# 48 units of u loaded ahead, gathers of u in steps 5 to 121 with up to seven buffers, each row multiplied one step after its fetch

## The chip, the cores and the metric

The kernel runs on one core of a Trainium2 chip. The metric is the device time of one execution in microseconds (us), taken as the median of several runs.

## The reference, cut to what matters

The kernel is one decoder layer over 256 tokens of width 2048. After an attention part and a LayerNorm, a retrieval part ("PEER") picks 128 experts for each token (8 heads of 16) out of 16384 and applies them:

```python
qh = (xc @ wq).reshape(PEER_CHUNK, PEER_HEADS, 2, PEER_HALF)
s1 = jnp.einsum('thd,kd->thk', qh[:, :, 0], sub_keys[0]).astype(jnp.float32)
s2 = jnp.einsum('thd,kd->thk', qh[:, :, 1], sub_keys[1]).astype(jnp.float32)
v1, i1 = lax.top_k(s1, PEER_TOPK)
v2, i2 = lax.top_k(s2, PEER_TOPK)
...
best, pos = lax.top_k(cand, PEER_TOPK)
expert = jnp.take_along_axis(cidx, pos, axis=-1)
gate = jax.nn.softmax(best, axis=-1)
u_sel = u[expert]
v_sel = v[expert]
act = jax.nn.gelu(jnp.einsum('td,thkd->thk', xc, u_sel).astype(jnp.float32), approximate=False)
return jnp.einsum('thk,thkd->td', (gate * act).astype(x.dtype), v_sel)
```

The change concerns the product of each token with the selected rows of u.

## The kernel before, in words

The product with u is made in two ways at once. For the first 1408 of the 2048 columns TensorE multiplies all tokens with all rows of u (the dense part). For the last 640 columns only the selected rows are fetched, by indirect DMA, and VectorE multiplies them with the token (the gathered part).

**The W_Q stage** comes first: 48 units (tiles of 128x512 floats, 256 KB each) of the query weights stream through four buffers named raw. Each unit is split into a high part (ScalarE, `hi`, L94) and a low part (`lo`, L95, on VectorE or, for units of odd number here, on GpSimd), and TensorE multiplies the tokens with both. In the same stretch VectorE and GpSimd find the best sixteen of each head (`retrieve`).

**The u stage** has 128 steps. A step takes 11 blocks of u, that is 2.75 units; 352 units in all. Each unit is split as above into one of four hi/lo pairs, each block takes three matmuls, and at the end of a step ScalarE copies the step's result from PSUM into the large tile S (L680). S has 64 places of one unit each; a place is filled with results as every second step ends, and until then it can hold a unit of u that was loaded ahead. A small planner (`place`, `follow`) decides when each unit is loaded into which place: a place may take a unit again once the one before it has been split, and only if no result is due there until the unit is used. The planner loads some units already in the W_Q stage (`PRE`), and two for each consumed unit after that as long as places are free. The last `RAW_END` units don't go through S but through the four raw buffers (L104).

**The gathers** are 256 indirect DMAs of 320 KB (128 rows of 640 floats), issued by GpSimd (L659) and spread evenly over the steps from `G0` up to `GE`. Their buffers rotate in the order of the program: `GB` = 3 of their own, and `GR` of every `GB + GR` from the raw buffers. VectorE multiplies each with the tokens' last 640 columns and sums (L684). The instructions that follow `issue_after` on VectorE may not stand ahead of the step's last split.

Loads are issued by SyncE in one queue; a load that waits for its buffer holds up those behind it. The framework orders each engine's instructions beforehand by an estimate of its own; loads and splits have a raised priority. After the u stage come the extraction of the gathered products and a stage of the same kind for v.

The knobs of the change: `PRE = (1, 2)` (a load ahead after every second W_Q unit), `RAW_END = 24`, `GR = 2`, `G0 = 12`, `GE = 125`.

Of the kernel before, what the change touches and what calls it, by code (L numbers as in the profile page):

```python
# [31 lines left out]
GU = D - KDU * P  # L32
# [6 lines left out]
UNIT = 512  # L39
EB = 8  # L40
GB = 3
GR = 2
GR_END = 128
RB = 4
RAW_END = 24
FIRST = 2
EARLY = 4
POOL_U = (1, 3)
# [1 line left out]
POOL_UE = 20  # L50
EARLY0 = 16
EARLY_N = 2
PRE = (1, 2)
BP = 3
AHEAD = 3000
G0 = 12
GE = 125
LEAD = 5
LAG = 1
KEEP0 = 40  # L60
# [11 lines left out]
def layer(ctx, tc, A, out):  # L72
# [11 lines left out]
    def bankA(name):  # L84
        return psA.tile([P, 512], F32, name=name, tag="a")
# [14 lines left out]
    def load_unit(src, raw=None, eng=None):  # L100
        with tc.high_priority(offset=AHEAD):
            if raw is None:
                raw = raw_unit()
                last_load[0] = nc.sync.dma_start(raw, src).ins  # L104
            pair = tuple(stream.tile([P, UNIT], F32R, name=s, bufs=4) for s in ("hi", "lo"))
            split(pair[0], pair[1], raw, eng)
        return pair
# [10 lines left out]
    def mm3(o, l, r, first, last):  # L118
        mm(o, l[0], r[0], start=first, stop=False)  # L119
        mm(o, l[0], r[1], start=False, stop=False)  # L120
        return mm(o, l[1], r[0], start=False, stop=last).ins  # L121
# [374 lines left out]
    def step_of(i2, sl=slice(0, T)):  # L496
        return S[:, i2 // 2, sl.start // 2:sl.stop // 2, i2 % 2, :]
# [4 lines left out]
    def s_part(p):  # L502
        return S[:, p].rearrange("p a b c -> p (a b c)")

    def paired(a):
        return a.rearrange("p (t j) -> p t j", j=2)
# [7 lines left out]
    for m in range(-WQ_UNITS, U_UNITS):  # L514
# [3 lines left out]
        n = max(n, m + 1)  # L518
        for _ in range((m * PRE[0] % PRE[1] < PRE[0]) if m < 0 else 2):
            fit = [p for p in free if 2 * p > (4 * n + 3) // KDU + 1]  # L520
            if n < U_UNITS - RAW_END and fit:
                place[n] = min(fit)
# [4 lines left out]
    def load_ahead(m):  # L527
        for n in follow[m]:
            p = place[n]
            with tc.issue_after(last_load[0]):  # L530
                last_load[0] = nc.sync.dma_start(s_part(p), A["u_d"][n]).ins

    count = [-WQ_UNITS]
# [117 lines left out]
    gorder = [(tt, h * PK + k) for h in range(HEADS) for k in range(PK) for tt in range(NT)]  # L651

    def gather(table, tt, slot, n):
        if table is A["u_g"] and slot < GR_END and count[0] % (GB + GR) >= GB:
            g = stream.tile([P, n], F32, name="g", tag="raw", bufs=RB)
        else:
            g = gath.tile([P, n], F32, name="g", bufs=GB)
        count[0] += 1
        nc.gpsimd.indirect_dma_start(out=g, out_offset=None, in_=table,  # L659
                                     in_offset=bass.IndirectOffsetOnAxis(ap=e_idx[:, tt, slot:slot + 1], axis=0))  # L660
        return g

    def spread(i, i0, i1):
        n = i1 - i0
        return gorder[len(gorder) * min(max(i - i0, 0), n) // n:len(gorder) * min(max(i - i0 + 1, 0), n) // n]

    after_unit[0] = None
    count[0] = 0
    w = None
    for i2 in range(P):  # L670
        ps = bankA("ups")[:, :T]
        for kt in range(KDU):
            un, k = divmod(i2 * KDU + kt, 4)
            if k == 0:
                p = place.get(un)
                w = load_unit(A["u_d"][un], None if p is None else s_part(p),
                              nc.gpsimd if un < POOL_UE and un % 4 in POOL_UU else None)
                load_ahead(un)
            mm3(ps, tuple(a[:, k * P:(k + 1) * P] for a in w), hs[kt], kt == 0, kt == KDU - 1)
        nc.scalar.copy(step_of(i2), paired(ps))  # L680
        with tc.issue_after(last_split[0]):
            for tt, slot in spread(i2, G0, GE):
                g = gather(A["u_g"], tt, slot, GU)
                nc.vector.scalar_tensor_tensor(g, g, 1.0, h_gath[:, tt], op0=ALU.mult, op1=ALU.mult,  # L684
                                               accum_out=pd[:, tt, slot:slot + 1])

# [92 lines left out]
    for m in range(P * NC):  # L779
        v_follow[m] = []  # L780
        i2, c = divmod(m, NC)
# [172 lines left out]
```

## Time and profile before

| what | value |
|---|---|
| median of 3 runs | 1747.99 us (1747.92 to 1755.24) |
| the profiled execution | 1756.99 us, span 1755.2 us |
| granted TensorE clock, mean | 0.984 |
| TensorE matmul busy | 1666.4 us (95%) |
| VectorE busy | 1450.0 us (83%) |
| ScalarE busy | 897.5 us (51%) |
| GpSimd busy | 886.7 us (51%) |
| the first and the last result copy of the u stage | at 500.30 and 1019.50 us |

The profile shows a single execution, whose own time is 9 us above the median. Busy times are shares of the whole span; the stages have different limits, so the u stage has to be read by itself.

### The profile page before, as it was taken

To read this page: it belongs to the slowest core of one execution; us is meant where nothing else is said; L and a number is where in the kernel's file an instruction comes from. 1 tells how busy PE (TensorE), PEld (TensorE's weight loads), DVE (VectorE), ACT (ScalarE), POOL (GpSimd) and SP (SyncE) were. 2 spreads that over 40 slices of the span, in tenths; PEclk is the share of its full clock that TensorE was granted. 3 is DMA by queue.
4 is the path that set the end of the run, shared out by engine and by line. 5 is a ranking of instruction groups with operands and counts; after the bars stand their busy time and mean duration, and the time that the engine had idled before them with its cause. 6 is when DMAs were issued, how large, how long until landed. Compare 5 with 4: busy or idle time off the path is not lost. (4 is left out here: it accounts for less than half of the span.)

```text
span 1755.2 us, 33099 instructions
## 1 busy us (share of the span) xinstructions
PE 1666.4 (95%) x10652; PEld 1484.7 (85%) x10652; DVE 1450.0 (83%) x3515; ACT 897.5 (51%) x1885; POOL 886.7 (51%) x899
## 2 busy tenths in 40 slices
PE   8999999989899999999999889988999999999996
PEld 8999888869888999999999788876687888888883
DVE  6766676679999888889888798877888888889896
ACT  6545565444344555555554358773454555555551
POOL 0000000036775656566565588856747645456562
PEclk9999999989999999999999999998999999999998
DMA  7667657726688999999999841137999999999962
GB/s 219 179 188 192 203 175 261 255 79 214 193 287 268 337 361 321 323 347 336 344 330 329 293 146 55 55 103 255 296 329 333 381 338 332 338 319 328 352 200 89
DMA packets 206014, 451.13 MB, mean 257 GB/s; under 512 B 26928, under 2 KB 31472, under 8 KB 205328
## 3 DMA queue, kind: packets, MB, share of 16 engines
q1 hardware_dynamic: 164816, 297.93, 51.4%
q0 software_dynamic: 41024, 151.09, 24.7%
q8 instruction: 84, 1.38, 0.3%
q14 instruction: 90, 0.74, 0.1%
HBM read 444.59 MB, written 4.26 MB: 256 GB/s over the span
## 5 line engine op out<-in xcount | busy, mean ns | idle before, releaser
L94 ACT CAST hi<-S 128x512 fp32r<-128x512 f32 x677 | 420.4, 622 | 450.5 <-PE vacc L121 223.2
L95 DVE TENSOR_TENSOR lo<-S,hi 128x512 fp32r<-128x512 f32 x672 | 464.5, 701 | 89.6 <-ACT hi L94 81.4
L121 PE MATMUL ups<-hTh,lo 128*128 128x256 f32 x1408 | 392.2, 283 | 11.7 <-DVE lo L95 11.1
L119 PE MATMUL ups<-hTh,hi 128*128 128x256 f32 x1408 | 392.2, 280 | 4.5 <-ACT hi L94 4.2
L120 PE MATMUL ups<-hTl,hi 128*128 128x256 f32 x1408 | 394.0, 281 | 0.0
L659 POOL DMA_INDIRECT g<-u_g,e_idx x256 | 289.2, 1130 | 173.1 <-DVE g L684 119.4
L94 ACT CAST hi<-raw 128x512 fp32r<-128x512 f32 x327 | 202.0, 621 | 245.4 <-PE projT L120 58.9
L95 DVE TENSOR_TENSOR lo<-raw,hi 128x512 fp32r<-128x512 f32 x303 | 216.6, 720 | 111.3 <-ACT hi L94 107.2
L120 PE MATMUL vacc<-lo,wt 128*128 128x512 f32 x744 | 278.4, 401 | 8.6 <-DVE lo L95 8.5
L121 PEld LDWEIGHTS ups<-hTh,lo 128*128 128x128 f32 x1408 | 263.5, 189 | 16.8 <-DVE lo L95 15.6
L121 PE MATMUL vacc<-hi,wt 128*128 128x512 f32 x744 | 276.2, 399 | 0.0
L119 PEld LDWEIGHTS ups<-hTh,hi 128*128 128x128 f32 x1408 | 266.0, 189 | 6.1 <-ACT hi L94 6.1
L120 PEld LDWEIGHTS ups<-hTl,hi 128*128 128x128 f32 x1408 | 265.7, 189 | 0.0
L119 PE MATMUL vacc<-hi,wt 128*128 128x512 f32 x744 | 231.2, 400 | 7.3 <-ACT wt L94 6.9
L805 POOL DMA_INDIRECT g<-v_g,e_idx x139 | 166.3, 1196 | 128.4 <-DVE accg L813 109.0
L684 DVE SCALAR_TENSOR_TENSOR g<-g,h_gath 128x640 f32<-128x640 f32 x256 | 204.9, 820 | 16.6 <-DMA g<-u_g,e_idx 16.1
L805 POOL DMA_INDIRECT raw<-v_g,e_idx x117 | 137.2, 1173 | 84.7 <-DVE accg L813 65.2
L120 PEld LDWEIGHTS vacc<-lo,wt 128*128 128x128 f32 x744 | 141.1, 190 | 45.7 <-DVE lo L95 12.0
L119 PEld LDWEIGHTS vacc<-hi,wt 128*128 128x128 f32 x744 | 141.2, 190 | 42.9 <-ACT wt L94 8.0
L121 PEld LDWEIGHTS vacc<-hi,wt 128*128 128x128 f32 x744 | 140.9, 189 | 34.5 <-issue 0.5
L714 POOL TENSOR_SCALAR bt<-cst,slotT 128x128 f32<-128x128 f32 x192 | 126.3, 675 | 23.3 <-POOL bt L714 16.4
L294 POOL TENSOR_TENSOR bias<-bias,score 128x128 f32<-128x128 f32 (+1 forms) x16 | 11.5, 739 | 233.1 <-DMA bias<-relb 115.8
(243 smaller groups left out, 3074.1 us busy)
## 6 DMA issues: line engine op xcount, KB each, us to landing
S<-v_d SPq DMA_DIRECT2D x361, 256.0 KB, 5.1
S<-u_d SPq DMA_DIRECT2D x328, 256.0 KB, 5.3
raw<-w_t SPq DMA_DIRECT2D x100, 256.0 KB, 2.8
raw<-w_n SPq DMA_DIRECT2D x64, 256.0 KB, 2.8
raw<-w_o SPq DMA_DIRECT2D x64, 256.0 KB, 3.3
raw<-w_q SPq DMA_DIRECT2D x48, 256.0 KB, 3.1
bc<-i_dram SPq DMA_DIRECT2D x32, 256.0 KB, 3.1
raw<-u_d SPq DMA_DIRECT2D x24, 256.0 KB, 5.1
```

The source lines that it names most:

```text
L94: last_copy[0] = nc.scalar.copy(hi, src).ins
L95: last_split[0] = (eng or nc.vector).tensor_tensor(lo, src, hi.bitcast(F32), op=ALU.subtract).ins
L119: mm(o, l[0], r[0], start=first, stop=False)
L120: mm(o, l[0], r[1], start=False, stop=False)
L121: return mm(o, l[1], r[0], start=False, stop=last).ins
L294: nc.gpsimd.tensor_tensor(bias[:, tt, :n], bias[:, tt, :n], sel[:, tt, :n], op=ALU.add)
L659: nc.gpsimd.indirect_dma_start(out=g, out_offset=None, in_=table, in_offset=bass.IndirectOffsetOnAxis(ap=e_idx[:, tt, slot:slot + 1], axis=0))
L684: nc.vector.scalar_tensor_tensor(g, g, 1.0, h_gath[:, tt], op0=ALU.mult, op1=ALU.mult, accum_out=pd[:, tt, slot:slot + 1])
L714: eng.tensor_scalar(bt[j][:, i], iota, i2T[:, t:t + 1], None, op0=ALU.is_equal)
L805: nc.gpsimd.indirect_dma_start(out=g, out_offset=None, in_=A["v_g"], in_offset=bass.IndirectOffsetOnAxis(ap=e_idx[:, tt, slot:slot + 1], a ...
```

## The change

Five knobs and one rule are altered. A unit of u is loaded ahead after each W_Q unit (48 of them, not 24). Only the last 12 units, not 24, go through raw. The gathers are spread over steps 5 to 121 (before: 12 to 124). Up to slot 96 (the first 192 gathers) they rotate through three buffers of their own and all four raw ones, after that through three and two (before: three and two throughout). And the row fetched in a step is multiplied in the step after it.

```diff
-GR = 2
-GR_END = 128
+GR = (4, 2)
+GR_END = 96
 RB = 4
-RAW_END = 24
+RAW_END = 12
...
-PRE = (1, 2)
+PRE = (1, 1)
...
-G0 = 12
-GE = 125
+G0 = 5
+GE = 122
...
-        if table is A["u_g"] and slot < GR_END and count[0] % (GB + GR) >= GB:
+        if count[0] % (GB + GR[slot >= GR_END]) >= GB:
             g = stream.tile([P, n], F32, name="g", tag="raw", bufs=RB)
...
-    w = None
+    w, fetched = None, []
     for i2 in range(P):
...
-            for tt, slot in spread(i2, G0, GE):
-                g = gather(A["u_g"], tt, slot, GU)
+            due, fetched = fetched, [(tt, slot, gather(A["u_g"], tt, slot, GU)) for tt, slot in spread(i2, G0, GE)]
+            for tt, slot, g in due:
                 nc.vector.scalar_tensor_tensor(g, g, 1.0, h_gath[:, tt], op0=ALU.mult, op1=ALU.mult,
                                                accum_out=pd[:, tt, slot:slot + 1])
```

## Rows read from the trace of the kernel before

**Rows 1.** Busy us: TensorE, weight loads, VectorE, ScalarE, GpSimd; clock, DMA share, GB/s

```profile
400.00:489.00 89.00, 81.14 (x649) 79.23 (x648) 86.98 (x339) 32.65 (x61) 64.96 (x76) 0.96 0.67 215
489.00:500.00 11.00, 8.37 (x59) 8.16 (x58) 11.00 (x35) 2.92 (x6) 9.67 (x11) 0.84 0.94 328
500.00:603.00 103.00, 98.47 (x808) 95.53 (x808) 97.28 (x282) 51.03 (x97) 68.09 (x77) 1.00 0.84 282
603.00:956.00 353.00, 353.00 (x3000) 353.00 (x2999) 308.01 (x639) 183.13 (x340) 218.01 (x193) 1.00 0.96 338
956.00:1020.00 64.00, 53.80 (x400) 49.34 (x398) 48.33 (x106) 23.26 (x46) 36.39 (x34) 0.97 0.89 296
```

**Rows 2.** Timeline of ScalarE: the result copies of steps 0, 24, 115 and 127

```profile
500.30 0.39 ACT L680 COPY S<-ups 128x256 f32<-128x256 f32 x1
...
603.00 0.39 ACT L680 COPY S<-ups 128x256 f32<-128x256 f32 x1
...
956.04 0.39 ACT L680 COPY S<-ups 128x256 f32<-128x256 f32 x1 [1.87 <-PE ups L121]
...
1019.50 0.40 ACT L680 COPY S<-ups 128x256 f32<-128x256 f32 x1 [1.99 <-PE ups L121]
```

**Rows 3.** Waits, 956 to 1020 us: total us, times, longest

```profile
ACT hi L94 <- DMA raw<-u_d: 20.6, 13, 3.9
...
DVE g L684 <- DMA g<-u_g,e_idx: 9.2, 11, 2.1
```

**Rows 4.** Waits, 400 to 489 us (W_Q stage)

```profile
ACT hi L94 <- DMA raw<-w_q: 27.7, 17, 3.7
```

**Rows 5.** Groups of VectorE, 405 to 553 us: busy us, mean ns, idle before

```profile
L95 DVE TENSOR_TENSOR lo<-raw,hi 128x512 fp32r<-128x512 f32 x22 | 20.6, 937 | 0.3 <-ACT hi L94 0.3
```

**Rows 6.** The multiplies (L684) from 489 to 603 us

```profile
L684 DVE SCALAR_TENSOR_TENSOR g<-g,h_gath x30: 810/817/857, 556.5 to 602.7; 128x640 f32<-128x640 f32 x30
```

**Rows 7.** Waits, 489 to 600 us

```profile
DVE g L684 <- DMA g<-u_g,e_idx: 3.7, 3, 2.4
```

**Rows 8.** Groups of VectorE and GpSimd, 600 to 950 us

```profile
L95 DVE TENSOR_TENSOR lo<-S,hi 128x512 fp32r<-128x512 f32 x249 | 169.6, 689 | 41.3 <-ACT hi L94 36.7 <-DMA S<-u_d 2.2
L684 DVE SCALAR_TENSOR_TENSOR g<-g,h_gath 128x640 f32<-128x640 f32 x192 | 153.8, 820 | 3.5 <-DMA g<-u_g,e_idx 3.2
...
L659 POOL DMA_INDIRECT g<-u_g,e_idx x193 | 219.1, 1135 | 132.9 <-DVE g L684 92.1 <-issue 39.0 <-DVE lo L95 1.8
```

**Rows 9.** Waits, 600 to 950 us

```profile
ACT hi L94 <- PE ups L120: 143.0, 212, 1.0
```

**Rows 10.** Timeline of VectorE, SyncE and ScalarE around units 325 and 327

```profile
956.97 0.69 DVE L95 TENSOR_TENSOR lo<-S,hi 128x512 fp32r<-128x512 f32 x1
...
957.69 0.33 SPq L531 DMA_DIRECT2D S<-u_d  x1
...
961.09 1.29 DVE L95 TENSOR_TENSOR lo<-S,hi 128x512 fp32r<-128x512 f32 x2 [1.94 <-ACT hi L94]
...
961.81 0.33 SPq L531 DMA_DIRECT2D S<-u_d  x1
...
965.29 0.69 DVE L95 TENSOR_TENSOR lo<-S,hi 128x512 fp32r<-128x512 f32 x1
...
965.69 0.62 ACT L94 CAST hi<-S 128x512 fp32r<-128x512 f32 x1 [0.75 <-DMA S<-u_d]
...
966.64 1.28 DVE L95 TENSOR_TENSOR lo<-S,hi 128x512 fp32r<-128x512 f32 x2
```

**Rows 11.** DMA issues of the whole span: KB each, median us to landing

```profile
S<-u_d SPq DMA_DIRECT2D x328, 256.0 KB, 5.3
raw<-w_t SPq DMA_DIRECT2D x100, 256.0 KB, 2.8
```

**Rows 12.** DMA issues, 960 to 1012 us

```profile
raw<-u_d SPq DMA_DIRECT2D x22, 256.0 KB, 5.0
```

**Rows 13.** Busy us by engine, 995 to 1000 us, columns as in Rows 1

```profile
995.00:1000.00 5.00, 2.99 (x15) 2.59 (x14) 3.92 (x10) 2.05 (x4) 3.97 (x4) 0.76 0.82 247
```

## The prediction

> **What bounds the kernel now.** I first cut the trace into stretches of busy time, to see which engine is full in which stage [rows 1]. In the W_Q stage (400 to 489 us) VectorE is busy 86.98 of 89 us and the DMA engines are two thirds used. From 500 to 603 VectorE is still at 97.28 of 103, because the selection of experts runs on into the u stage, and TensorE has small gaps. From 603 to 956 TensorE is busy 353 of 353 us: nothing else matters there. From 956 to 1020 TensorE falls to 53.80 of 64, and no other engine is full.
>
> Second, the result copies give the pace [rows 2]. Between the copies of steps 24 and 115 lie 353.04 us for 91 steps, 3.88 us a step, 1.41 us a unit. By that pace the first 24 steps should take 93.1 us and take 102.7: 9.6 us lost at the front. The last 12 should take 46.6 and take 63.5: 16.9 lost in the tail. The loss at the front lies where VectorE is full. For the tail the waits tell the cause [rows 3]: ScalarE waits 20.6 us for units in raw, and VectorE 9.2 us for gathered rows. Raw is short of buffers: 24 units and the gathers share four.
>
> So the change can win only in the tail and at the front; and it can lose in the W_Q stage, at the front and in the tail.
>
> **The change part by part.** *24 more loads in the W_Q stage.* They move 24 x 256 KB ahead, each in SyncE's queue before a load of W_Q that until now had none before it. At the 338 GB/s of the middle stretch [rows 1] one takes 0.78 us, all 18.6 us: room enough, as a third of 89 us is free. W_Q's loads behind them land later by up to 0.78 us each, and ScalarE waits for these loads already, 27.7 us in 17 waits [rows 4]. Behind ScalarE wait the low parts and TensorE. Lower bound 0, upper bound 18.6 us, if every delay reaches TensorE. The nearest row decides: with those 27.7 us of waits, VectorE's low parts waited for ScalarE only 0.3 us [rows 5], since VectorE's own queue is the longer one. I take 1.0 us.
>
> *Multiplies from step 6 instead of 12.* Up to step 24 the old program has 13 x 2.265 = 29 multiplies due, and the trace has them (30 up to 602.7) [rows 6]: they keep to their program place. The new one has due (24 - 5) x 2.188 = 41.6, so 12 more at 0.83 us a piece (820 ns, and part of the 82 ns read of the sum), 10.0 us more on a VectorE with 103 - 97.28 = 5.7 us free. If all that is free can be used, 4.3 us are left over and delay the low parts queued behind, and so TensorE. If none, 10.0; if the multiplies slip behind the selection and are made up in the middle, nothing. Against it, the waits of VectorE for gathered rows in this stretch, 3.7 us [rows 7], can end, since a row now has a step (3.88 us) longer to land. Between -3.7 and +10.0 I take +2.4 us, the middle between 4.3 (the multiplies at their place, the waits as now) and 0.6 (the waits all gone).
>
> Here a rule of the Trainium skill speaks against the change. The rows say: the low part takes 689 ns in the middle, where GpSimd does nothing but issue indirect DMAs [rows 8], and 937 ns before 553 us, where GpSimd computes too [rows 5]. GPSIMD Engine Reference, section "1. Specifications", says that GpSimd shares its SBUF interfaces with VectorE and that instructions with two SBUF inputs, as the low part, contend. If issuing gathers did this, the 52 units of steps 6 to 24 would lose 0.25 us each, 13 us; by the row of the middle they lose nothing. The trace agrees with the rule for computing, not for issuing, and the sum goes by the row.
>
> *Seven buffers and the later multiply in the middle.* Nothing is won: TensorE has no gap there. What hides it is VectorE's reserve, 308 of 353 us busy, and ScalarE being ahead of TensorE (143 us of waiting for it) [rows 1, 9]. GpSimd's 92 us of waiting for free buffers [rows 8] lie behind this cover. If it were gone, each late row would hold up VectorE's queue and the low parts in it, as in the tail. Taken: 0.
>
> *The tail.* Gathers end at step 121 and multiplies at 122, so the last 12 units, from step 123 on, have raw to themselves. But units 328 to 339 now go through S, where fewer places are free as the end nears. Working the planner's loop through: its lead was four units or more for all units up to 327; now units 329 to 331 are issued three units ahead, 332 to 337 two, and 338 and 339 one. Place 63 holds 324, 328, 331, 333, 335, 337, 338 and 339 in turn: seven links, each from the end of one low part to the end of the next. A link's price is read around two old loads [rows 10]. Unit 327: the low part before it on its place ends at 961.73, its load is issued at 961.81, its high part starts at 965.69, its low part ends at 967.92: 6.2 us. Without the time it queued on VectorE: 0.08 + 3.88 + 0.62 + 0.69 = 5.3. Unit 325: from 957.66 to 965.98, 8.3 us, since several multiplies stood before its low part. Without gathers beside it, the landing would be as for W_T, 2.8 us, not 5.0 to 5.3 [rows 11, 12]: 4.2 us.
>
> TensorE needs unit 339 at 15 x 1.41 = 21.2 us after 324, and has a reserve of 2.8: a high part starts when TensorE is done four units earlier [rows 9], three units (4.2 us) before its turn, less 1.4 for both parts. With 6.2 for the first two links, 5.3 for two more as long as gathers run, and 4.2 for the last three, the chain takes 35.6 us: 35.6 - 21.2 - 2.8 = 11.6 lost, where 16.9 were: -5.3 us. With 4.2 throughout, 5.4 are lost: -11.5. With 8.3 for the four contended links, 21.8: +4.9. After 339 no loss follows: 340 to 343 already lie in raw, and four buffers at 4.2 us give a unit every 1.05 us. So the wait for raw gives way to one for places; it is only shorter.
>
> **The sum.** +1.0 + 2.4 + 0 - 5.3 = -1.9 us, on the profiled execution's own 1757.0 (span 1755.2 and 1.8 around it) 1755.1. The runs' median is 9.0 below the profiled one; on it the sum gives **1746 us**. About 0.5%, 8.7 us, is what a measurement of this kernel can tell from no change.
>
> **The rivals.** *The tail clears and the front doesn't suffer* (for it: the waits for rows end, landings shorten; against: one place for 338 and 339): +1.0 + 0 - 11.5 = -10.5, 1737; with the front's -3.7, 1734. Chance 0.34.
>
> *W_Q is delayed* (the other side): a load in the queue and on the engines before each late load of W_Q. For it: the 27.7 us; against: VectorE's 0.3. It decides once more than 11.6 of the 18.6 us reach TensorE; all of it gives 18.6 + 2.4 - 5.3 = +15.7, 1764. Chance 0.10.
>
> *The places cost more than raw did*: contended links at 8.3: +1.0 + 2.4 + 4.9 = +8.3, and with a low clock as between 995 and 1000, where after several waits 0.76 was granted, a mean of the levels 1.2 and 2.4 GHz, and 0.24 x 5 = 1.2 us went [rows 13], +9.5: 1757.5. Chance 0.08.
>
> *Gathers slow the low parts at the front*: 13 us as worked out above, +11.1 in all, 1759. Chance 0.06. The page named above would have it so; the middle stretch speaks against it.
>
> **How the numbers follow.** My forecast, no change that can be told, has 0.42, with a range of its own from 1739 to 1757; faster 0.34; slower 0.10 + 0.08 + 0.06 = 0.24. The range for 8 in 10 leaves out a tenth on each side: down past the faster rival's 1734 to 1731, as front and tail may both be at their low ends (-14.2 in sum), and up to 1763, where W_Q's delay nearly has its full price.
>
> **What would show it.** Right: the copies of steps 115 and 127 about 58 us apart (now 63.5), with ScalarE waiting for S, not raw, in steps 119 to 123, two waits of some 3 us before units 338 and 339, and no gap after; VectorE's waits for gathered rows near zero; from 603 to 956 TensorE as full as now; the first copy some 1 us later, VectorE full for longer. Wrong: a tail as long as now or with no waits; the first copy more than 5 us later; multiplies that only start after 550 us; or gaps of TensorE in the middle.

## The result and the profile after

The changed kernel is slower: 1767.7 us median of 5 runs (1765.4 to 1769.9) against 1750.6 (1747.9 to 1755.2), ratio 1.0094 with a 95% interval of 1.0074 to 1.0114, 17 us. The profiled execution took 1767.7 us, span 1765.9.

The stretches of busy time after, cut at the same points of the program as [rows 1] (columns as there):

```profile
400.00:489.00 89.00, 77.79 (x637) 75.01 (x636) 86.39 (x332) 32.20 (x60) 63.82 (x75) 1.00 0.82 273
489.00:502.00 13.00, 10.13 (x70) 9.72 (x70) 13.00 (x45) 3.53 (x7) 11.19 (x14) 0.87 1.03 383
502.00:607.00 105.00, 99.31 (x800) 97.09 (x799) 98.33 (x282) 50.36 (x96) 68.69 (x77) 0.97 0.68 225
607.00:962.00 355.00, 354.61 (x3007) 354.06 (x3006) 310.68 (x642) 182.30 (x340) 222.79 (x196) 1.00 0.95 336
962.00:1033.00 71.00, 55.77 (x397) 51.46 (x395) 47.28 (x103) 23.84 (x45) 28.75 (x29) 0.90 0.80 254
```

The loads ahead did what they say: the DMA engines' share rose from 0.67 to 0.82 in the W_Q stage and fell from 0.84 to 0.68 in the front of the u stage. Yet TensorE lost its time where it lost it before, in the last stretch, and more of it: 55.77 busy of 71 us, the DMA engines less used and the clock lower than in [rows 1].

The result copies of steps 0, 24, 115 and 127, on ScalarE's timeline:

```profile
502.04 0.39 ACT L680 COPY S<-ups 128x256 f32<-128x256 f32 x1
...
607.05 0.40 ACT L680 COPY S<-ups 128x256 f32<-128x256 f32 x1 [0.56 <-PE ups L121]
...
962.08 0.39 ACT L680 COPY S<-ups 128x256 f32<-128x256 f32 x1 [2.33 <-PE ups L121]
...
1032.69 0.39 ACT L680 COPY S<-ups 128x256 f32<-128x256 f32 x1 [3.46 <-PE ups L121]
```

Against [rows 2]: the first copy is 1.7 us later, steps 0 to 24 take 105.0 us (102.7 before), 24 to 115 355.0 (353.0), 115 to 127 70.6 (63.5): 1.7 + 2.3 + 2.0 + 7.2 = 13.2 us. From there to the end of the span the changed kernel took 733.2 us, the old one 735.7, so this pair of profiles differs by 10.7 us only, where the runs differ by 17. The old kernel's profiled execution was a long one: 1757.0 us, where its runs in this study had medians from 1750.6 to 1753.9.

The waits from 962 to 1033 us, to be laid beside [rows 3]:

```profile
ACT hi L94 <- DMA S<-u_d: 25.2, 14, 5.0
...
DVE g L684 <- DMA g<-u_g,e_idx: 9.3, 10, 2.1
```

ScalarE no longer waits for units in raw (20.6 us) but for units in S (25.2), and VectorE waits for gathered rows as long as before (9.2), though each is multiplied a step later.

The chain on place 63: the low parts of units 324, 328, 331, 333, 335, 337, 338 and 339 on VectorE, with the loads (SyncE) and the high parts (ScalarE) of the last two (where a line merges two or three low parts, the chain's is the last):

```profile
967.53 0.69 DVE L95 TENSOR_TENSOR lo<-S,hi 128x512 fp32r<-128x512 f32 x1 [0.64 <-ACT hi L94]
...
972.96 1.88 DVE L95 TENSOR_TENSOR lo<-S,hi 128x512 fp32r<-128x512 f32 x3
...
982.12 1.29 DVE L95 TENSOR_TENSOR lo<-S,hi 128x512 fp32r<-128x512 f32 x2
...
990.40 0.69 DVE L95 TENSOR_TENSOR lo<-S,hi 128x512 fp32r<-128x512 f32 x1
...
995.43 0.69 DVE L95 TENSOR_TENSOR lo<-S,hi 128x512 fp32r<-128x512 f32 x1 [2.23 <-ACT hi L94]
...
999.67 0.69 DVE L95 TENSOR_TENSOR lo<-S,hi 128x512 fp32r<-128x512 f32 x1
...
1000.39 0.33 SPq L531 DMA_DIRECT2D S<-u_d  x1
...
1004.50 0.62 ACT L94 CAST hi<-S 128x512 fp32r<-128x512 f32 x1 [4.87 <-DMA S<-u_d]
...
1005.55 0.69 DVE L95 TENSOR_TENSOR lo<-S,hi 128x512 fp32r<-128x512 f32 x1
...
1006.27 0.33 SPq L531 DMA_DIRECT2D S<-u_d  x1
...
1010.46 0.62 ACT L94 CAST hi<-S 128x512 fp32r<-128x512 f32 x1 [3.34 <-DMA S<-u_d]
...
1011.11 0.69 DVE L95 TENSOR_TENSOR lo<-S,hi 128x512 fp32r<-128x512 f32 x1
```

Each load of the pair is issued 0.03 us after the low part before it ends (1000.36 and 1000.39, 1006.24 and 1006.27): nothing but the place is waited for. The low parts end at 968.22, 974.84, 983.41, 991.09, 996.12, 1000.36, 1006.24 and 1011.80; the links take 6.6, 8.6, 7.7, 5.0, 4.2, 5.9 and 5.6 us, 43.6 in all. Most of a link is the landing of its load. The loads of units 328 to 339 on this place, with KB and us from issue to landing:

```profile
S<-u_d SPq DMA_DIRECT2D x1, 256.0 KB, 4.8
S<-u_d SPq DMA_DIRECT2D x1, 256.0 KB, 6.2
S<-u_d SPq DMA_DIRECT2D x1, 256.0 KB, 5.7
S<-u_d SPq DMA_DIRECT2D x1, 256.0 KB, 3.6
S<-u_d SPq DMA_DIRECT2D x1, 256.0 KB, 2.8
S<-u_d SPq DMA_DIRECT2D x1, 256.0 KB, 4.0
S<-u_d SPq DMA_DIRECT2D x1, 256.0 KB, 4.1
```

Together the seven landings take 31.2 of the 43.6 us.

### The profile page after: what moved, and what is told of

The parts are those of the page before. It is cut to its first block, busy times and chain, and to the rows that moved or that the text cites. A ratio compares the mean times of both kernels' runs of the same rounds, so it can differ in the third digit from the quotient of the medians.

```text
span 1765.9 us, 33095 instructions
## 1 busy us (share of the span) xinstructions
PE 1668.1 (94%) x10652; PEld 1484.6 (84%) x10652; DVE 1448.8 (82%) x3515; ACT 896.5 (51%) x1885; POOL 884.1 (50%) x899
## 5 line engine op out<-in xcount | busy, mean ns | idle before, releaser
L94 ACT CAST hi<-S 128x512 fp32r<-128x512 f32 x689 | 426.9, 622 | 461.6 <-PE vacc L121 209.0
L95 DVE TENSOR_TENSOR lo<-S,hi 128x512 fp32r<-128x512 f32 x684 | 472.0, 695 | 100.8 <-ACT hi L94 97.2
L94 ACT CAST hi<-raw 128x512 fp32r<-128x512 f32 x315 | 194.6, 621 | 228.3 <-PE projT L120 57.0
L95 DVE TENSOR_TENSOR lo<-raw,hi 128x512 fp32r<-128x512 f32 x291 | 209.3, 722 | 114.7 <-ACT hi L94 112.7
L805 POOL DMA_INDIRECT g<-v_g,e_idx x139 | 162.5, 1169 | 123.1 <-DVE accg L813 101.6
L684 DVE SCALAR_TENSOR_TENSOR g<-g,h_gath 128x640 f32<-128x640 f32 x256 | 207.9, 820 | 11.8 <-DMA g<-u_g,e_idx 11.7
L805 POOL DMA_INDIRECT raw<-v_g,e_idx x117 | 144.4, 1234 | 88.8 <-DVE accg L813 67.2
L813 DVE SCALAR_TENSOR_TENSOR accg<-g,pd,accg 128x512 f32<-128x512 f32 x139 | 107.4, 775 | 27.6 <-DMA g<-v_g,e_idx 26.9
```

The source lines that it names most:

```text
L94: last_copy[0] = nc.scalar.copy(hi, src).ins
L95: last_split[0] = (eng or nc.vector).tensor_tensor(lo, src, hi.bitcast(F32), op=ALU.subtract).ins
L805: nc.gpsimd.indirect_dma_start(out=g, out_offset=None, in_=A["v_g"], in_offset=bass.IndirectOffsetOnAxis(ap=e_idx[:, tt, slot:slot + 1], a ...
L813: nc.vector.scalar_tensor_tensor(accg[:, tt], g, pd[:, tt, slot:slot + 1], accg[:, tt], op0=ALU.mult, op1=ALU.add)
```

## The experiments

My theory was that the places of S, held by the units that used to go through raw, make the loss (called *places* below). The rivals were the early start of the gathers (*front*) and the loads ahead in the W_Q stage. All ratios are against the kernel before on the same chip; the table gives times between result copies in one profiled execution each, in us (0 to 24 is the front, 115 to 127 the tail).

| kernel | ratio, 95% interval | first copy | 0 to 24 | 24 to 115 | 115 to 127 | last copy |
|---|---|---|---|---|---|---|
| before | 1 | 500.3 | 102.7 | 353.0 | 63.5 | 1019.5 |
| the change | 1.0094, 1.0074 to 1.0114 | 502.0 | 105.0 | 355.0 | 70.6 | 1032.7 |
| before_raw12 | 1.0075, 1.0056 to 1.0094 | 501.2 | 102.6 | 353.0 | 71.3 | 1028.1 |
| after_raw24 | 1.0043, 1.0028 to 1.0058 | 500.9 | 105.0 | 351.8 | 51.1 | 1008.8 |
| after_g0_12 | 1.0041, 1.0028 to 1.0054 | 502.0 | 99.3 | 351.1 | 70.8 | 1023.2 |
| after_pre12 | 1.0105, 1.0090 to 1.0120 | 501.8 | 109.4 | 349.7 | 69.9 | 1030.8 |
| before_buffers | 1.0020, 1.0006 to 1.0035 | 502.4 | 100.1 | 351.9 | 64.9 | 1019.2 |
| before_g0_5 | 1.0043, 1.0025 to 1.0060 | 501.5 | 110.0 | 353.3 | 62.3 | 1027.2 |
| after_g12_raw18 | 0.9976, 0.9963 to 0.9988 | 502.5 | 99.3 | 351.1 | 58.5 | 1011.4 |
| after_cut | one run | 501.0 | 104.1 | 352.2 | 64.7 | 1022.0 |
| before_raw18 | 1.0021, 1.0009 to 1.0033 | 504.1 | 101.4 | 349.7 | 66.3 | 1021.5 |
| after_g12_raw18_now | 0.9983, 0.9966 to 1.0000 | 499.5 | 101.4 | 351.6 | 57.3 | 1009.8 |
| after_raw18 | 1.0019, 0.9999 to 1.0038 | 502.1 | 102.8 | 351.8 | 58.7 | 1015.4 |
| after_g12_raw20 | 1.0014, 1.0002 to 1.0025 | 501.2 | 99.7 | 351.1 | 57.4 | 1009.4 |

The column 24 to 115 shows more than the edits. In the 50 us from 700 to 750 us TensorE is busy without a gap at a granted clock of 1.00 in every kernel, and yet it runs in one of two rhythms, here in the kernel before and in after_g0_12:

```profile
700.00:750.00 50.00, 50.00 (x427) 50.00 (x426) 43.02 (x90) 26.01 (x48) 29.96 (x28) 1.00 0.92 323
...
700.00:750.00 50.00, 50.00 (x431) 50.00 (x430) 44.16 (x93) 26.52 (x49) 31.38 (x28) 1.00 0.96 343
```

The kernel before, the change, before_raw12 and before_g0_5 have the slower one (427 matmuls), the other ten the faster (430 or 431). On 353 us that makes 3.3 us (4 of 431). What sets the rhythm is open, so differences of this size in that column are not put down to an edit here.

**before_raw12**, the places alone:

```diff
-RAW_END = 24
+RAW_END = 12
```

> The kernel before with one knob of the change: the last 12 units through raw, not 24, so that units 328 to 339 pass through the last free places of S. Theory (places): the tail loses by this alone; copies of steps 115 to 127 about 70 us apart instead of 63.5, ratio to before 1.004 to 1.006. Rivals (the front's row of multiplies, or the loads in the W_Q stage, make the loss): no difference, ratio 0.999 to 1.001.

The tail grew to 71.3 us and the ratio is 1.0075, more than I had expected: this one knob costs by itself most of what the change costs. The rivals, by which nothing would happen, are out as the only cause.

**after_raw24**, the places taken back:

```diff
-RAW_END = 12
+RAW_END = 24
-GR = (4, 2)
+GR = (4, 2, 0)
 GR_END = 96
+GR_OFF = 122
...
-        if count[0] % (GB + GR[slot >= GR_END]) >= GB:
+        if count[0] % (GB + GR[(slot >= GR_END) + (slot >= GR_OFF)]) >= GB:
```

> The changed kernel with the last 24 units through raw again; so that no unit waits for a row whose multiply stands behind it, the gathers from slot 122 on take only the three buffers of their own. Theory (places): the tail comes back to 64 us or less from 70.6, ratio to before about 1.005 instead of 1.009. Rivals: tail as in the changed kernel, ratio 1.008 to 1.010.

The tail of the dense part is the shortest of all, 51.1 us, and half of the loss is gone. But only half: the last 12 gathers, in three buffers, trail, and the last multiply ends at 1028.7 us, 20 us behind the last copy. The extraction needs both. So the tail has two ends, the dense units and the gathers, which compete for raw.

**after_g0_12**, the front taken back:

```diff
-G0 = 5
+G0 = 12
```

> The changed kernel with gathers from step 12 on, as before (110 steps up to 121). Theory (places): tail stays at 70 us or more, ratio 1.007 to 1.010, the front wins at most the 2 to 3 us that steps 0 to 24 lost. Rival (front): the row of seven multiplies at step 14 goes, steps 0 to 24 take 102 us or less instead of 105 and the whole loss of 17 us shrinks to half or less, ratio 1.004 or below.

My theory missed here and the rival hit: the tail is as long as in the change (70.8), but steps 0 to 24 fell to 99.3 us and the ratio to 1.0041, where the rival had 1.004 or below. Two causes, then. VectorE's timeline of the changed kernel shows the second:

```profile
557.88 0.82 DVE L684 SCALAR_TENSOR_TENSOR g<-g,h_gath 128x640 f32<-128x640 f32 x1
...
562.35 0.82 DVE L684 SCALAR_TENSOR_TENSOR g<-g,h_gath 128x640 f32<-128x640 f32 x1
562.35 0.08 DVE L684 DVE_READ_ACCUMULATOR g<-g,h_gath 128x1 f32 x1
...
563.10 1.29 DVE L95 TENSOR_TENSOR lo<-S,hi 128x512 fp32r<-128x512 f32 x2
```

and TensorE's, what waits for the low part:

```profile
563.84 0.58 PE L121 MATMUL ups<-hTh,lo 128*128 128x256 f32 x1 [3.00 <-DVE lo L95]
```

Seven multiplies, one for each buffer, stand in a row from 557.88 to 563.10. Their rows had been asked for between 484.7 and 500.4 us, but the multiplies start only behind the last instruction of the selection on VectorE, at 557.58 us. The low parts queued behind them, and step 14 took 8.3 us, step 15 5.7. With gathers from step 12 the same engine shows two multiplies between pairs of low parts:

```profile
557.89 0.82 DVE L684 SCALAR_TENSOR_TENSOR g<-g,h_gath 128x640 f32<-128x640 f32 x1
...
558.63 0.82 DVE L684 SCALAR_TENSOR_TENSOR g<-g,h_gath 128x640 f32<-128x640 f32 x1
...
559.38 1.29 DVE L95 TENSOR_TENSOR lo<-S,hi 128x512 fp32r<-128x512 f32 x2
```

Only half of those two steps' loss is the wait itself. From 563 to 570 us the clock was granted at 0.51, close to its lower level, and TensorE made 29 matmuls in the changed kernel, where after_g0_12 made 62 at 1.00 (columns as in [rows 1]):

```profile
563.00:570.00 7.00, 6.16 (x29) 6.17 (x30) 4.96 (x12) 1.64 (x3) 5.46 (x6) 0.51 0.84 269
...
563.00:570.00 7.00, 7.00 (x62) 7.00 (x61) 7.00 (x16) 3.53 (x7) 5.47 (x6) 1.00 0.98 335
```

The wait stands at this place in all six kernels of the table with gathers from step 5 (2.0 us in after_cut, 3.0 in the others) and in none of the eight with gathers from step 12. The clock in these 7 us was below 1.00 in five of the six; in before_g0_5, after the same 3.0 us, it stayed at 1.00.

**after_pre12**, the W_Q stage taken back:

```diff
-PRE = (1, 1)
+PRE = (1, 2)
```

> The changed kernel with a load ahead after every second W_Q unit, as before (24 units). Theory (places): only the 1.7 us of the first result copy come back, ratio 1.008 to 1.010. Rival (W_Q's loads delayed): first copy at 500 us or earlier and ratio 1.005 or below. If the 24 loads helped the front, it gets slower than the changed kernel.

Not faster, if anything slower, and the first copy hardly moved (501.8): the loads ahead don't make the loss. Without them steps 0 to 24 took 109.4 us, 4.4 more than with them; before_g0_5, which also has 24 loads ahead, shows 110.0. So far as single profiles tell, the loads ahead shorten the front when the gathers start early.

**before_buffers**, the buffers and the loads ahead alone:

```diff
-GR = 2
-GR_END = 128
+GR = (4, 2)
+GR_END = 96
-PRE = (1, 2)
+PRE = (1, 1)
...
-        if table is A["u_g"] and slot < GR_END and count[0] % (GB + GR) >= GB:
+        if count[0] % (GB + GR[slot >= GR_END]) >= GB:
```

> The kernel before with 48 units loaded ahead and with up to seven buffers (four raw ones up to slot 96), but gathers in steps 12 to 124, the last 24 units through raw and each row multiplied in its own step. Theory (places and the early start make the loss): no loss, steps 0 to 100 a few us shorter than before (394 instead of 397), tail 63 to 65 us, ratio 0.995 to 1.000. Rival (the buffers or the loads ahead themselves cost): ratio above 1.003.

Steps 0 to 100 took 392.7 us instead of 397.4, somewhat less than expected, but the tail took 1.4 us more. The ratio, 1.0020, lies between what theory and rival had and is a miss for both: buffers and loads ahead win nothing in this tail, and lose little.

**before_g0_5**, the early start alone:

```diff
-G0 = 12
+G0 = 5
```

> The kernel before with gathers from step 5 on only (120 steps up to 124). Theory (the early start fills VectorE's queue with rows in a row behind the selection): steps 0 to 24 take 105 us or more instead of 102.7, the tail gains at most 1 to 2 us from the lower rate, ratio 1.001 to 1.004. Rival (only places): ratio 0.997 to 1.000.

The front loses here without any places: steps 0 to 24 take 110.0 us, ratio 1.0043, as after_g0_12 had it from the other side. The row of seven multiplies is here too (the gathers take all four raw buffers in turn in this kernel as well), and TensorE waits 1.1 to 1.7 us three times more by the copy of step 24.

**after_g12_raw18**, both mended in part:

```diff
-G0 = 5
+G0 = 12
-RAW_END = 12
+RAW_END = 18
-GR = (4, 2)
+GR = (4, 2, 0)
 GR_END = 96
+GR_OFF = 126
...
-        if count[0] % (GB + GR[slot >= GR_END]) >= GB:
+        if count[0] % (GB + GR[(slot >= GR_END) + (slot >= GR_OFF)]) >= GB:
```

> The changed kernel with gathers from step 12 on and the last 18 units through raw: units 334 to 339 leave the two last places, and the last 4 gathers use only their own buffers. Theory (places): the six shortest links go, tail of 70.8 falls to 60 us or less, ratio to before 0.998 to 1.001 against 1.004 with 12. Rival (the tail is bound by the gathers, not the places): tail as long, or the multiplies trail behind the last copy, ratio 1.003 or more.

The tail fell from 70.8 to 58.5 us and the ratio from 1.0041 to 0.9976: 0.24% faster than the kernel before (0.12 to 0.37%). Its copies of steps 115 and 127:

```profile
952.90 0.39 ACT L681 COPY S<-ups 128x256 f32<-128x256 f32 x1 [2.85 <-PE ups L122]
...
1011.39 0.39 ACT L681 COPY S<-ups 128x256 f32<-128x256 f32 x1 [2.80 <-PE ups L122]
```

**after_cut**, the changed kernel without its last 16 gathers and multiplies, their products left at zero:

```diff
+    nc.vector.memset(pd, 0.0)
...
-... for tt, slot in spread(i2, G0, GE)]
+... for tt, slot in spread(i2, G0, GE) if slot < 120]
```

> The changed kernel without its last 16 gathers and their multiplies (slots 120 to 127; their products stay zero), so that no gather runs beside units 328 to 339. If the links of the chain of places cost what they do because of the gathers, loads land in some 2.8 us, links fall to 4.2 us and the copies of steps 115 to 127 are 52 to 54 us apart, not 70.6. If the places themselves set it (landing and handing over), 62 us or more.

The last low parts of the chain (units 337, 338, 339) on VectorE:

```profile
993.37 0.69 DVE L95 TENSOR_TENSOR lo<-S,hi 128x512 fp32r<-128x512 f32 x1 [0.77 <-ACT hi L94]
...
997.51 0.69 DVE L95 TENSOR_TENSOR lo<-S,hi 128x512 fp32r<-128x512 f32 x1 [3.45 <-ACT hi L94]
...
1001.62 0.69 DVE L95 TENSOR_TENSOR lo<-S,hi 128x512 fp32r<-128x512 f32 x1 [3.42 <-ACT hi L94]
```

and the loads there, KB and median us to landing, in this kernel (985 to 1003 us):

```profile
S<-u_d SPq DMA_DIRECT2D x4, 256.0 KB, 2.7
```

and in the changed one (995 to 1010 us), with the gathers beside them:

```profile
S<-u_d SPq DMA_DIRECT2D x3, 256.0 KB, 4.0
...
g<-u_g,e_idx POOLq DMA_INDIRECT x6, 4.1
```

With no gather beside them loads land in 2.7 us and the last two links take 4.1 us each, about as I had priced them; with gathers the loads of the last two links took 4.0 and 4.1 us, the links 5.9 and 5.6. But the tail came down only to 64.7 us, not to 52 to 54, so by what I had written the places themselves set it. The run doesn't settle that, for its gathers trail: the last one belongs to step 114, whose copy came at 953.4 us, and was issued at 977.3, and loads of the extraction (bc) followed from 978.3. The first four links, beside these, took 7.4, 5.5, 6.2 and 6.9 us, the fifth 4.7. Without the last 16 gathers, then, the tail lost 6 us less of its 24, in one run; how the other 18 divide between the hand-overs on the last places and traffic beside their loads is not shown.

**before_raw18**, a middle dose on the kernel before:

```diff
-RAW_END = 24
+RAW_END = 18
```

> The kernel before with only the last 18 units through raw, not 24 (the change has 12). Theory (a tail set by how many buffers units have: 4 raw ones shared with gathers on one side, the last places of S on the other): fewest losses in between, copies of steps 115 to 127 at 57 to 62 us, below both 63.5 (24) and 71.3 (12), ratio 0.996 to 0.999. Rival (every unit moved from raw to places costs): 66 to 68 us, ratio 1.003 to 1.004.

A miss: 66.3 us, where the rival had 66 to 68, and a ratio of 1.0021, between theory and rival. Step 125 alone took 12.1 us. SyncE's waits, 995 to 1022 us:

```profile
SPq L104 <- DVE g L684: 6.6, 2, 4.7
```

A load for raw waits 4.7 us for a multiply: in this kernel gathers take raw buffers up to step 124, among the units. In after_g12_raw18 the gathers have left raw by then, and the same 18 units have a tail of 58.5 us; that kernel differs in its loads ahead and its buffers too, so the gathers in raw are the likely reason, not a separated one.

**after_g12_raw18_now**, without the later multiply:

```diff
-            due, fetched = fetched, [(tt, slot, gather(A["u_g"], tt, slot, GU)) for ...]
+            due = [(tt, slot, gather(A["u_g"], tt, slot, GU)) for ...]
```

> The kernel with gathers from step 12 and 18 units through raw, but each row multiplied in its own step. If the later multiply is worth something, more waits for gathered rows in the tail and a ratio of 1.000 or more instead of 0.998; if it is worth nothing, 0.997 to 0.999.

Ratio 0.9983 against 0.9976, intervals overlapping, and VectorE's waits for gathered rows in the tail are 6.4 us against 6.1: the later multiply is worth nothing that can be told.

**after_raw18**, the tail mended, the early start kept:

```diff
-G0 = 12
+G0 = 5
```

(against after_g12_raw18)

> The changed kernel with the last 18 units through raw and the last 4 gathers in their own buffers, gathers from step 5 on as in the change. If places and early start add up, it stands between: ratio 1.002 to 1.005 (the early start's 0.5% over 0.998), steps 0 to 24 at 104 to 106 us, tail at 58 to 60. If the early start costs only together with the long tail, 0.997 to 0.999.

1.0019, between 1.0094 and 0.9976 and at the lower edge of what I expected. The early start costs 0.43% here, 0.43% alone (before_g0_5) and 0.53% beside the long tail: within the intervals the two causes add up. Steps 0 to 24 were 102.8 us, 3.5 above the 99.3 of the kernel with step 12, below what I expected.

**after_g12_raw20**, two units more through raw:

```diff
-RAW_END = 18
+RAW_END = 20
-GR_OFF = 126
+GR_OFF = 124
```

(against after_g12_raw18)

> Gathers from step 12 and the last 20 units through raw (the last 8 gathers in their own buffers). Units 332 and 333 leave the two last places too. Theory (places): tail 58 us or a little less, ratio 0.996 to 0.998. Rival (the last gathers in three buffers trail): last multiply after the last copy, ratio 1.000 or more.

The rival hit: the dense tail is 57.4 us, as the theory had it, but the multiplies end 14 us behind the last copy (1009.4) and the ratio is 1.0014. The multiplies of this kernel, first and last start:

```profile
L685 DVE SCALAR_TENSOR_TENSOR g<-g,h_gath x256: 812/818/973, 557.5 to 1022.9; 128x640 f32<-128x640 f32 x128
```

## Why the prediction was wrong

**The sum.** By the pair of profiles, term by term: the W_Q stage +1.0 forecast and +1.7 measured, the front +2.4 and +2.3, the middle 0 and +2.0, the tail -5.3 and +7.2, what follows the last copy 0 and -2.5. The tail is nearly the whole miss there. By runs, of 1752 us, the places cost 0.75% (before_raw12 alone; and the step from 1.0094 to 1.0019, where after_raw18 has six units fewer in places), 13 us; the early start 0.43 to 0.53% (1.0043 alone; 1.0094 to 1.0041; 1.0019 to 0.9976), 8 to 9 us. Together 21 to 22 us, from which the rest of the change takes back some 4 (after_g12_raw18, which has the rest of it and a mended tail, stands at -4): 17. The steps from 1.0094 over 1.0019 to 0.9976 are one difference cut in two, so they must add up; the check is that before_raw12 and before_g0_5, each edit alone, cost as much.

**The tail was the step that failed.** The chain of places was the right mechanism, with the right units and hand-overs; the term that was mis-sized is the landing of the loads in it. I priced the seven links at 35.6 us with 23.9 us of landing (3.88 for four loads, 2.8 for three); they took 43.6 with 31.2 of landing, so landing is 7.3 of the 8.0 us. There are two errors in it. For the contended links I took 3.88 us from one load, unit 327's, where the median of the same loads stood in [rows 11] with 5.3; the first three took 4.8, 6.2 and 5.7. And for the last two I let the gathers end at step 121 by the clock. They end at step 121 of the program, and as TensorE waits, the multiplies, and with them the gathers, wait with it: the last multiply ended at 1011.1 us, just before the low part of 339 began. These two loads took 4.0 and 4.1 us; after_cut, without gathers beside its last two, shows 2.7. A stall stretches whatever is tied to the steps.

By my own formula the measured links give 43.6 - 21.2 - 2.8 = 19.6 us lost; the tail lost 70.6 - 46.6 = 24.0. In the 4.4 us that remain TensorE's clock had fallen, after a wait of 3.3 us before unit 338 and two of 1.4 before 339 (0.50 is its lower level, 1.2 of 2.4 GHz):

```profile
1000.00:1005.00 5.00, 1.86 (x16) 1.65 (x14) 2.22 (x6) 0.50 (x1) 3.05 (x3) 1.00 0.80 244
1005.00:1010.00 5.00, 2.81 (x13) 2.02 (x13) 4.22 (x11) 0.52 (x2) 1.16 (x1) 0.69 0.78 237
1010.00:1015.00 5.00, 3.84 (x16) 3.46 (x17) 3.53 (x7) 2.53 (x6) 0.00 (x0) 0.50 0.86 301
1015.00:1020.00 5.00, 5.00 (x36) 5.00 (x36) 2.08 (x3) 2.11 (x5) 0.00 (x0) 0.79 0.57 138
```

The Trainium skill, TensorE: Matmul & The Clock Gate, section "HAM oscillation — how this bites in real kernels", says that waits for DMA between bursts of matmuls let the clock fall again; the trace agrees. My estimate from these rows: half of 3.84 us in the third, and 0.21 of 5 us in the fourth, 3.0 of the 4.4 us. It is argued, no run took the clock away, and the other 1.4 us stay open. My rival "the places cost more than raw did" came nearest to this tail, with +9.5 us in all; I gave it 0.08.

**The front.** Its +2.4 came out at +2.3 in the profiles, and that is luck. The early start alone made steps 0 to 24 longer by 5.7 us (105.0 against 99.3 in after_g0_12), and the rest of the change made them shorter by 3.4 (99.3 against 102.7), a gain that I had not counted. Three cases were named: multiplies at their place, all in the way, or slipping behind the selection "and made up in the middle, nothing". They slipped: the first started at 557.9 us, a sign that I had named as wrong, and 31 had started by the copy of step 24, where 42 were due; the 30 of [rows 6] had not kept their program place either, for none had started before 556.5. But what slipped was made up in a row of seven, as many as there were buffers, and that held up the low parts for 5.2 us and TensorE for 3.0, and the low clock behind that wait cost about as much again (an estimate: half of the 6.16 us of TensorE in 563 to 570 us). Slipping isn't free when the queue keeps its order. The waits for gathered rows, which I let end, went from 3.7 us [rows 7] to 2.4.

**The rule on GpSimd's port** that I weighed did nothing, as I took it: two low parts right behind that row took 1.29 us together while gathers were being issued, as pairs in [rows 10] do.

**The W_Q stage.** +1.0 was taken and the first copy came 1.7 us later. ScalarE's waits for W_Q's loads grew from 27.7 us [rows 4] to 40.4, and VectorE stayed as full as it was (86.39 of 89 us). But the first copies of all kernels lie between 499.5 and 504.1 us, those with 24 loads ahead from 500.3, those with 48 up to 502.5. So no cost of the loads can be told, and the 1.7 us don't confirm the 1.0.

**Buffers and later multiply in the middle**: 0, and TensorE was full there as forecast. The change took 2.0 us more there; both kernels have the slower rhythm, and the 2.0 are not explained.

**The chances** treated the rivals as alternatives. The front and the tail failed together. With only one of the two mended or made, the medians lie inside or just above my range, whose end is 1763: before_g0_5 1760.4, after_g0_12 1758.5, after_raw24 1760.3, before_raw12 1765.3.

**Open.** The pair of profiles shows 10.7 us, the runs 17. The old kernel's profiled execution was one of its longer ones, some 5 us above its median of 1752, and in which stage isn't known; so the tail of before_raw12 is 7.9 us longer by profiles, the kernel 13.9 by runs. The part after the u stage (the span less the last copy) takes between 731.4 and 745.3 us. It is longest in after_raw24 and after_g12_raw20 (745.0 and 745.3), whose multiplies trail; the others, up to 741.5, are in no order that goes with their edits. Why that part varies wasn't tried. The rhythm of the matmuls is open too: after_g0_12 has the faster one and the change the slower, so 3.3 of the 9.3 us between their profiles may not be the early start's.

## What to carry to other kernels

When a shared buffer is short near the end of a stage, look for all who hold it: here units and gathered rows competed for raw, and moving units to places that run out only moved the wait. The kernel that won (0.9976) moves only a few of them and has the gathers out of raw before the last units come. A chain of one-deep buffers is priced link by link, each a whole load, landing and split; take the landing from the median under the traffic that will be beside it, not from one quick load. Work tied to the same steps goes on beside the chain for as long as the chain stalls. Work started earlier on an engine that is full needn't run earlier: here it ran later in one piece, ahead of what others waited for. And a term that comes out right may be two wrong ones: take the edits one by one.

## What the runs showed of the hardware

A load of 256 KB landed in 2.7 us (median) with no gather beside it; in the chain of the changed kernel, with gathers, in 2.8 to 6.2 us, and in 4.0 and 4.1 near its end, where the DMA engines' mean share was only 0.78 to 0.80.

TensorE's clock fell to its lower level after a few waits of 1.4 to 3.3 us, though TensorE had worked in between. After the single wait of 3.0 us at step 14 it fell in some kernels (0.51 and 0.76 over 563 to 570 us) and not in before_g0_5 (1.00).

With TensorE busy without a gap at a granted clock of 1.00, the same matmuls ran at 427 or at 430 to 431 in 50 us, by the kernel's profile; what sets this is open.
